# A block of two FFNs and a mixer on one Trainium2 core: half of x's quadrant sums move into the output projection, and the second FFN goes from four plain blocks and nine pairs to two and ten

## The chip, the core and the metric

The kernel runs on one core of a Trainium2 chip. The metric is device time in microseconds (us) of one execution, as the median of several runs; lower is better. The core has a matrix engine (PE, with its weight loads shown as PEld), VectorE (DVE), ScalarE (ACT), GpSimd (POOL) and SyncE (SP). Each works through its own queue in program order and waits on semaphores of the others; SP and POOL issue the DMAs here. Matrix products land in banks of PSUM; everything else lies in SBUF.

## What is computed

One layer on x of 512 tokens by 1024 features, float32: a half-weighted FFN, a mixer of two attentions, a second half-weighted FFN, and a norm.

```python
x = x + 0.5 * swiglu(rmsnorm(x, norm_ffn1), w_ffn1_gate, w_ffn1_up, w_ffn1_down)
x = x + hybrid_mixer(rmsnorm(x, norm_mix), w_in, ..., w_out, rel_bias)
x = x + 0.5 * swiglu(rmsnorm(x, norm_ffn2), w_ffn2_gate, w_ffn2_up, w_ffn2_down)
return rmsnorm(x, norm_final)
# swiglu(h, g, u, d) = (silu(h @ g) * (h @ u)) @ d, with 2816 hidden columns
```

## The kernel before

**Layout.** x is held transposed as eight tiles `x0` to `x7` of 128 features by 512 tokens. In the built program and in the trace they are `x_70` to `x_77`. Every factor of a product is split in two (`halves`, lines 76 to 93, and `halves_of_x`, line 210): ACT writes a rounded copy (`whi`, `sph`, `xo`, `th`), and the difference goes to `wlo`, `spl`, `xo`, `tl`. Three matmuls (`mm3`, lines 95 to 98) then stand for one product. The difference is taken by DVE, except for the weights loaded during the mixer, where POOL takes it in pieces of 128 columns (line 89).

**FFN.** The 2816 hidden columns are 22 blocks of 128. A *plain* block (line 244) multiplies gate and up weights with all 512 tokens: 48 matmuls of 512 columns. A *pair* (line 283) does two blocks at once by Strassen's scheme in Winograd's form. The weights are quartered by input half and block, x by input half and token half, and seven products of 24 matmuls with 256 columns replace eight. A pair's operands include sums of weight quarters (S1 to S4, DVE, line 299) and sums of x's quadrants (T1 to T4). The sums of x are the same for all pairs. `sums_of_x(k)` (line 192) makes them for k = 0 to 3 from the tiles `x[k]` and `x[k+4]`: ACT writes two gained copies into `xa`, DVE makes four sums into `xv`, and two splits follow, a narrow one of 256 columns for T1 and a wide one of 768 for the others. Plain blocks do not need them, so each FFN starts with four plain blocks, and the sums are made beside these (`begun`, line 441, after its steps 3, 7, 9 and 11). A pair's products add up in three PSUM banks `u`, `v`, `w`. The first product in `u` is copied away by ACT into `wc` (line 317), and the third product of the pair then adds onto the same bank.

**Norm.** The root of the mean square scales the FFN's results, not its input. For the second FFN POOL adds up the squares of x's tiles in `acc` (line 148); after step 2 PE sums them over features (`pr`), after step 4 it spreads the roots into rows (`pR`), and ACT copies these to `R` (line 167). Only then can a block be finished (`finish`, line 268, or `c12` and `c21`): two products with `R` on DVE, silu on ACT, a product, and the split into `h`.

**Down projection.** After a part of the hidden columns (`PARTS`, line 23) its down products are stepped in between the steps of later pairs, at places given by `SLOTS` and `FEWER` (`mixed`, line 398). After the first four blocks, eight down steps (`LEAD`) stand in one run before the pairs. A result tile in PSUM (`pd`) is added to x by DVE where its number is even. Where it is odd, ACT copies it to `acc`, and POOL sends a DMA that adds it to x (`half_sent`, line 495).

**Output projection.** `w_out` (line 845) multiplies the heads' outputs `oT` with `w_o` for eight tiles d, first k = 4 to 7 among the attention steps, then k = 0 to 3 at the end in the order 0, 1, 2, ... 7 (`last`, line 1067). Its PSUM tiles `pw` use the tag `mm`, which has two banks. `ended` (line 839) drains a bank: DVE adds it to x (line 840), then follow the gained split of x (`gained`, lines 132 and 133) and the square. Tiles 0 and 1 are held until the last head is done (`held`), and both finish together.

**Order.** PE's order is the order in which the program is written (`manual_schedule`). The queues of DVE, ACT, POOL and SP are set at build time by a scheduler that estimates durations. A tile from a pool (`tile_pool`) waits for the last user of what lay at its place. The mixer's pool for heads, `ap`, is closed with the mixer, and the FFN's pools are opened after that.

Of the kernel before, what the change touches and what calls it, by code (L numbers as in the profile page):

```python
# [21 lines left out]
PLAIN = 4  # L22
PARTS = (0, 4, 6, 10, 14, 18, 22)
# [5 lines left out]
LEAD = 8  # L29
AHEAD = ((0, 26.0, True), (0, 22.0, False), (1, 12.8, None), (2, 8.6, None))  # L30
SLOTS = (0, 1, 2, 3, 4, 5, 6, 7, 9, 12, 15, 18, 21, 23, 25, 27)
FEWER = (0, 1, 2, 3, 4, 5, 6, 7, 12, 16, 20, 24)


@with_exitstack
def block_kernel(ctx: ExitStack, tc: tile.TileContext, A: dict, out: bass.AP):
# [144 lines left out]
    class Ffn:  # L181


        def __init__(self, w, which, tmp, hp, sp):
            self.w, self.which, self.tmp, self.hp, self.sp = w, which, tmp, hp, sp
            self.xg, self.hs, self.early, self.cuts, self.halved = None, {}, {}, (), NF
            self.behind = made[0]
            self.t1 = [[xp.tile([128, S], F32R, name="xo", tag="xo", bufs=20) for _ in range(2)] for _ in range(2)]
            self.th, self.tl = [sp.tile([128, 4, 3, HT], F32R, name=n, tag=n, bufs=1) for n in ("th3", "tl3")]
            nc.gpsimd.memset(sp.tile([128, 16], F32, name="gap", tag="gap", bufs=1), 0.0)  # L190

        def sums_of_x(self, k):
            ab, v = [self.sp.tile([128, 4, 2, 128], F32, name=n, tag=t, bufs=3).rearrange("p a b c -> p (a b c)")
                     for n, t in (("xa", "sph"), ("xv", "spl"))]
# [6 lines left out]
            nc.vector.tensor_tensor(t1, a1, a2, ALU.subtract)  # L201
            nc.vector.scalar_tensor_tensor(t2, t1, -1.0, b2, ALU.mult, ALU.subtract)
            nc.vector.scalar_tensor_tensor(t4, t2, -1.0, b1, ALU.mult, ALU.subtract)
            nc.vector.tensor_tensor(t3, b2, a2, ALU.subtract)
# [78 lines left out]
        def pair(self, f):  # L283
# [9 lines left out]
            def sums(name):  # L293

                a11, a12, a21, a22 = [A[i, j] for i in range(2) for j in range(2)]
                to, x, y, op = {"S1": (a21, a21, a22, ALU.add), "S2": (a11, a21, a11, ALU.add),
                                "S3": (a11, a11, a22, ALU.subtract), "S4": (a12, a11, a12, ALU.add)}[name]
                with after(self.behind_lo):
                    nc.vector.tensor_tensor(to, x, y, op)  # L299
# [98 lines left out]
        def mixed(self, steps, fills):  # L398
# [103 lines left out]
    with ExitStack() as ph:  # L502
# [10 lines left out]
        ffn = Ffn(A["wgu1"], 0, tmp, hp, sp)  # L513
# [52 lines left out]
        def then(d, p):  # L566
# [13 lines left out]
        steps += ffn.mixed(pairs, fills) + ffn.down(A["wd1"][f:], fs, then, None, 4)  # L580
# [8 lines left out]
    with ExitStack() as ph:  # L589
        tmp = ph.enter_context(tc.tile_pool(name="tmp2", bufs=2))  # L590
        kv = ph.enter_context(tc.tile_pool(name="kv", bufs=1))
        ap = ph.enter_context(tc.tile_pool(name="ap", bufs=2))
# [244 lines left out]
        out_done = set()  # L837

        def ended(d, p, k0):
            nc.vector.tensor_tensor(xs[d], p, xs[d], ALU.add)  # L840
# [226 lines left out]
        last = [w_out(d, 0, 4, both if d < 2 else None) for d in range(NK)]  # L1067
# [66 lines left out]
        with tc.manual_schedule(engines={mybir.EngineType.PE}):  # L1134
            for i in range(len(steps) + 9):
# [9 lines left out]
        xg = [got["x", d] for d in range(NK)]  # L1145
# [3 lines left out]
    with ExitStack() as ph:  # L1149
        tmp = ph.enter_context(tc.tile_pool(name="tmp3", bufs=5))  # L1150
        hp = ph.enter_context(tc.tile_pool(name="hp3", bufs=2))
        sp = ph.enter_context(tc.tile_pool(name="sp3", bufs=2))
        ffn = Ffn(A["wgu2"], 2, tmp, hp, sp)
        ffn.xg = xg
        hs = ffn.hs
        ffn.halved = PARTS[-2]
# [4 lines left out]
        for f, end in zip(PARTS[1:], PARTS[2:]):  # L1161
# [4 lines left out]
        ffn.go(steps + ffn.mixed(pairs, fills))  # L1166
# [42 lines left out]
        last = range(PARTS[-2], NF)  # L1209
# [68 lines left out]
def _down(w):  # L1278
# [4 lines left out]
    for f, end in zip(PARTS, PARTS[1:]):  # L1283
# [5 lines left out]
def _laid_out(x, norm_ffn1, w_ffn1_gate, w_ffn1_up, w_ffn1_down, norm_mix, w_in, cmp_pos_k, cmp_w1_k,  # L1289
# [17 lines left out]
        "x": c(x[0]), "wd1": _down(w_ffn1_down[0]),  # L1307
# [6 lines left out]
        "wd2a": _down(w_ffn2_down[0])[:PARTS[-2]],  # L1314
        "wd2b": _blocks(w_ffn2_down[0][PARTS[-2] * 128:], F - PARTS[-2] * 128, S),
# [27 lines left out]
```

## Time and profile before

| | |
|---|---|
| median of 3 runs | 974.65 us (973.8 to 975.12) |
| profiled execution | 973.68 us, of which the span from first to last instruction is 971.9 us |
| mean granted PE clock | 0.999 |
| busy share of the span | PE 99%, PEld 88%, DVE 75%, ACT 55%, POOL 22% |
| last tiles of the output projection drained | 605.05 (x0, x1) to 625.62 us (x7) |
| first matmul of the second FFN | 622.04 us |
| first transpose of the tail (line 1178) | 940.23 us |

Times of trace rows are microseconds from the span's start. A timeline row gives start, duration, engine, line, operation, output and inputs, and in square brackets how long the engine stood idle before it and who released it. An operation that waits inside the engine shows it as a longer duration, with no bracket. Consecutive DVE and ACT operations start a little before the recorded end of the one ahead (the rows show 0.05 to 0.1 us).

### The profile page before, as it was taken

Reading aid. Unit: us, or ns where it says so; the run is one execution under the profiler, and the core shown is the slowest. Engines: PE = TensorE matmul, PEld = TensorE weight load, DVE = VectorE, ACT = ScalarE, POOL = GpSimd, SP = SyncE. Lnnn points to the kernel's source line nnn. Section 1 sums busy time; section 2 is a strip of 40 time slices with the busy share of each in tenths; the row PEclk is TensorE's granted clock in tenths of the full one; section 3 lists DMA queues with packets and bytes.
Section 4 is the critical chain, followed back from the end, with each engine's and each line's share of the span. In section 5 each row is a group of like instructions: output and inputs, shape, how many; then the busy total and the mean of one; then the engine's idle time right before and its main releaser. Section 6 shows DMA issues by size and latency. Waiting matters only on the chain.

```text
span 971.9 us, 16008 instructions
## 1 busy us (share of the span) xinstructions
PE 961.8 (99%) x6096; PEld 858.3 (88%) x6096; DVE 729.1 (75%) x1090; ACT 532.4 (55%) x893; POOL 217.8 (22%) x365
## 2 busy tenths in 40 slices
PE   9999999999999999999999999999999999999997
PEld 6889999999999898888888888888999999999986
DVE  5977787788776576678888885778678888777853
ACT  7844555454443445577676674674455554444534
POOL 0010010110001144236566564801001010100000
PEclk9999999999999999999999999999999999999999
DMA  8643574534532335662243531464446433445112
GB/s 311 241 136 93 173 223 137 157 107 105 135 83 65 85 101 163 202 195 62 70 109 98 131 99 54 152 216 120 121 119 163 127 97 115 118 132 153 44 22 87
DMA packets 51361, 124.39 MB, mean 128 GB/s; under 512 B 10673, under 2 KB 15234, under 8 KB 51284
## 3 DMA queue, kind: packets, MB, share of 16 engines
q1 hardware_dynamic: 39476, 91.62, 30.4%
q0 software_dynamic: 11520, 31.46, 13.5%
q8 instruction: 48, 0.79, 0.3%
q10 hardware_dynamic: 288, 0.27, 0.1%
q14 instruction: 29, 0.24, 0.1%
HBM read 100.08 MB, written 5.30 MB: 108 GB/s over the span
## 4 chain that ended last, share of the span: by engine, by line
PE 92%; DMA 3%; DVE 2%; issue 1%; POOL 1%; ACT 0%; SPq 0%; DVEq 0%; ACTq 0%
PE pd L97 8%; PE pd L96 8%; PE pd L98 8%; PE pu L98 7%; PE pu L97 7%; PE pu L96 7%; PE pw L96 5%; PE pw L97 5%; PE pw L98 5%; PE ps_t L976 3%; PE pv L96 3%; PE pv L98 3%; PE pv L97 3%; PE pp L96 3%; PE pgu L98 2%; PE pp L97 2%
## 5 line engine op out<-in xcount | busy, mean ns | idle before, releaser
L211 ACT ACTIVATE sph<-aw 128x1024 fp32r<-128x1024 f32 x128 | 133.7, 1059 | 147.1 <-PE pu L97 60.9
L212 DVE TENSOR_TENSOR spl<-aw,sph 128x1024 fp32r<-128x1024 f32 x128 | 155.0, 1223 | 57.2 <-ACT sph L211 57.1
L84 ACT ACTIVATE whi<-raw 128x1024 fp32r<-128x1024 f32 (+3 forms) x107 | 103.7, 971 | 98.9 <-PE pd L97 53.5
L500 POOL DMA_DIRECT2D x<-acc x40 | 35.0, 875 | 460.6 <-ACT acc L499 460.6
L96 PE MATMUL pd<-h,whi 128*128 128x512 f32 x320 | 126.5, 395 | 0.3 <-DVE x L493 0.3
L97 PE MATMUL pd<-h,whi 128*128 128x512 f32 x320 | 126.6, 396 | 0.0
L98 PE MATMUL pd<-h,wlo 128*128 128x512 f32 x320 | 125.8, 393 | 0.0
L91 DVE TENSOR_TENSOR wlo<-raw,whi 128x1024 fp32r<-128x1024 f32 (+3 forms) x83 | 102.9, 1243 | 28.0 <-ACT whi L84 27.3
L98 PE MATMUL pu<-th,spl 128*128 128x256 f32 x432 | 119.3, 276 | 0.0
L96 PE MATMUL pu<-th,sph 128*128 128x256 f32 x432 | 119.2, 276 | 0.0
L97 PE MATMUL pu<-tl,sph 128*128 128x256 f32 x432 | 119.2, 276 | 0.0
L299 DVE TENSOR_TENSOR aw<-aw 128x1024 f32<-128x1024 f32 x72 | 87.8, 1219 | 3.5 <-DMA aw<-in_wgu 3.2
L96 PEld LDWEIGHTS pu<-th,sph 128*128 128x128 f32 x432 | 81.1, 188 | 4.2
L97 PEld LDWEIGHTS pu<-tl,sph 128*128 128x128 f32 x432 | 81.1, 188 | 4.0
L98 PEld LDWEIGHTS pu<-th,spl 128*128 128x128 f32 x432 | 81.1, 188 | 0.0
L98 PE MATMUL pw<-xo,spl 128*128 128x256 f32 x288 | 79.6, 276 | 0.0
L96 PE MATMUL pw<-xo,sph 128*128 128x256 f32 x288 | 79.5, 276 | 0.0
L97 PE MATMUL pw<-xo,sph 128*128 128x256 f32 x288 | 79.5, 276 | 0.0
L89 POOL TENSOR_TENSOR wlo<-raw,whi 128x128 fp32r<-128x128 f32 x128 | 60.9, 508 | 60.8 <-DVE m L954 31.1
L98 PEld LDWEIGHTS pd<-h,wlo 128*128 128x128 f32 x320 | 60.1, 188 | 13.3
L96 PEld LDWEIGHTS pd<-h,whi 128*128 128x128 f32 x320 | 60.1, 188 | 3.8 <-DVE x L493 0.7
L97 PEld LDWEIGHTS pd<-h,whi 128*128 128x128 f32 x320 | 60.1, 188 | 2.5
(258 smaller groups left out, 2534.6 us busy)
## 6 DMA issues: line engine op xcount, KB each, us to landing
aw<-in_wgu SPq DMA_DIRECT2D x72, 512.0 KB, 4.8
raw<-in_wd POOLq DMA_DIRECT2D x22, 512.0 KB, 4.2
x<-acc POOLq DMA_DIRECT2D x40, 256.0 KB, 3.3
raw<-in_wd2a POOLq DMA_DIRECT2D x18, 512.0 KB, 4.1
raw<-in_w_a SPq DMA_DIRECT2D x16, 512.0 KB, 3.6
raw<-in_wgu SPq DMA_DIRECT2D x15, 512.0 KB, 4.3
raw<-in_w SPq DMA_DIRECT2D x8, 512.0 KB, 5.1
kvn<-xo SPq DMA_DIRECT2D x32, 128.0 KB, 2.4
```

What stands on the lines that cost most here:

```text
L84: nc.scalar.activation(hi[:, s], src[:, s], AF.Copy)
L89: nc.gpsimd.tensor_tensor(lo[:, i, b], src[:, i, b], f32(hi[:, i, b]), ALU.subtract)
L91: nc.vector.tensor_tensor(lo[:, s], src[:, s], f32(hi[:, s]), ALU.subtract)
L96: nc.tensor.matmul(p, w[0], v[0], start=first, stop=False, skip_group_check=again)
L97: nc.tensor.matmul(p, w[0], v[1], start=False, stop=False, skip_group_check=again)
L98: nc.tensor.matmul(p, w[1], v[0], start=False, stop=last, skip_group_check=again)
L211: nc.scalar.activation(hi, v, AF.Copy)
L212: nc.vector.tensor_tensor(lo, v, f32(hi), ALU.subtract)
L299: nc.vector.tensor_tensor(to, x, y, op)
L500: nc.gpsimd.dma_start(xs[d], acc, accum_op=ALU.add)
L976: nc.tensor.transpose(p[:, wide:wide + 128], lps[qi][:, j * 128:(j + 1) * 128], ident)
```

## The change

The second FFN has two plain blocks and ten pairs in place of four and nine; the first FFN stays as it is. The sums of x for k = 0 and 1 are made inside the output projection, as soon as tiles 4 and 5 are drained; those for k = 2 and 3 after the plain steps 3 and 2. To that end the end of the output projection runs in the order 0, 4, 1, 5, 2, 3, 6, 7 (0 and 4 held). `pR` comes after step 6 and not 4. No down steps stand in one run before the pairs, and the first part's down steps are put into the first pair from its step 8 on (`FIRST`). The mixer's head tiles go to the right end of SBUF and are given up before the last output tiles, so that `th3`, `tl3` and the copies `xa` and `xv` of the two early sums can lie there. The pool of the weights' tiles (`sp3`) is opened ahead of that for `h`.

```diff
-PLAIN = 4
-PARTS = (0, 4, 6, 10, 14, 18, 22)
+PARTS = ((0, 4, 6, 10, 14, 18, 22), (0, 2, 4, 6, 10, 14, 18, 22))
+FIRST = (8, 9, 10, 11, 12, 13, 14, 15, 17, 19, 21, 23)
...
-                if i % 28 in (FEWER if i < 84 else SLOTS) and fills and fills[0][0] <= i:
+                if i % 28 in slots[min(i // 28, len(slots) - 1)] and fills and fills[0][0] <= i:
...
-        sums = [(at, lambda k=k: ffn.sums_of_x(k)) for k, at in enumerate((3, 7, 9, 11))]
+        sums = [(at, lambda k=k: ffn.sums_of_x(k)) for k, at in sums]
...
-        return steps + fills[:LEAD], [(0, step) for step in fills[LEAD:]]
+        return steps + fills[:lead], [(0 if lead else 8, step) for step in fills[lead:]]
...
-        ap = ph.enter_context(tc.tile_pool(name="ap", bufs=2))
+        heads = ph.enter_context(ExitStack())
+        ap = heads.enter_context(tc.tile_pool(name="ap", bufs=2, side="right"))
...
                 squares(tmp, d, "t", 6)
+                later[d] = made[0]
+                if d in (4, 5):
+                    ffn.behind = later[d]
+                    ffn.sums_of_x(d % 4, xt)
...
-        last = [w_out(d, 0, 4, both if d < 2 else None) for d in range(NK)]
+        last = [w_out(d, 0, 4, both if d in (0, 4) else None) for d in (0, 4, 1, 5, 2, 3, 6, 7)]
...
+            heads.close()
+            tp = ctx.enter_context(tc.tile_pool(name="tp3", bufs=1, side="right"))
+            xt = ph.enter_context(tc.tile_pool(name="xt", bufs=2, side="right"))
+            ffn = Ffn(A["wgu2"], 2, tp)
             for _ in work:
                 pass
...
+        sp = ph.enter_context(tc.tile_pool(name="sp3", bufs=2))
         hp = ph.enter_context(tc.tile_pool(name="hp3", bufs=2))
-        sp = ph.enter_context(tc.tile_pool(name="sp3", bufs=2))
...
-            (2, lambda: roots(2, sums_of_squares("mm"))), (4, lambda: rows_of_roots(2, "mm"))])
+            (2, lambda: roots(2, sums_of_squares("mm"))), (6, lambda: rows_of_roots(2, "mm"))], 2, 0, ((2, 0), (3, 1)))
...
-        ffn.go(steps + ffn.mixed(pairs, fills))
+        ffn.go(steps + ffn.mixed(pairs, fills, (FIRST, FEWER, FEWER, FEWER, SLOTS)))
```

DVE's queue at the end of the output projection, before. `x<-pw` is the drain of a bank, `xo<-x,gcol,xo` the gained split.

```order
L840 TENSOR_TENSOR x_71<-pw,x_71 128x512
L133 SCALAR_TENSOR_TENSOR xo<-x_70,gcol,xo 128x512
L133 SCALAR_TENSOR_TENSOR xo<-x_71,gcol,xo 128x512
L840 TENSOR_TENSOR x_72<-pw,x_72 128x512
L133 SCALAR_TENSOR_TENSOR xo<-x_72,gcol,xo 128x512
L840 TENSOR_TENSOR x_73<-pw,x_73 128x512
L133 SCALAR_TENSOR_TENSOR xo<-x_73,gcol,xo 128x512
L840 TENSOR_TENSOR x_74<-pw,x_74 128x512
```

The same place now, from the third drain to the fifth. `xv` and `tl` rows belong to the sums of x for k = 0.

```order
L845 TENSOR_TENSOR x_71<-pw,x_71 128x512
L203 TENSOR_TENSOR xv<-xa 128x256
L206 TENSOR_TENSOR xv<-xa 128x256
L204 SCALAR_TENSOR_TENSOR xv<-xv,xa 128x256
L205 SCALAR_TENSOR_TENSOR xv<-xv,xa 128x256
L214 TENSOR_TENSOR xo<-xv,xo 128x256
L845 TENSOR_TENSOR x_75<-pw,x_75 128x512
L132 SCALAR_TENSOR_TENSOR xo<-x_71,gcol,xo 128x512
L214 TENSOR_TENSOR tl_6846<-xv,th_6845 128x768
L132 SCALAR_TENSOR_TENSOR xo<-x_75,gcol,xo 128x512
L845 TENSOR_TENSOR x_72<-pw,x_72 128x512
```

Between two drains stood one split; now five operations stand between the third and the fourth drain, three between the fourth and the fifth, and (not shown) four between the fifth and the sixth.

ACT's queue from the copy of `R` on, before: the first finished block follows at once, among sums of x.

```order
L167 ACTIVATE R<-pR 128x512
L272 ACT_TABLE_LOAD
L272 ACTIVATE t<-t 128x512
L84 ACTIVATE whi<-raw 128x1024
L231 ACTIVATE h<-t 128x512
```

The same place now: `sph` is a split of pair weights (ahead of `R` that of S2), `t` the silu of a plain block, `wc<-pu` the copy of the first pair's first product.

```order
L213 ACTIVATE sph<-aw 128x1024
L166 ACTIVATE R<-pR 128x512
L274 ACT_TABLE_LOAD
L274 ACTIVATE t<-t 128x512
L83 ACTIVATE whi<-raw 128x1024
L274 ACTIVATE t<-t 128x512
L233 ACTIVATE h<-t 128x512
L213 ACTIVATE sph<-aw 128x1024
L319 ACTIVATE wc<-pu 128x512
```

The copy of `R` and both blocks' silus now stand between the pair's first splits and the copy that its third product needs.

More of the change, by code (lines that the diff above doesn't have):

```diff
@@ L1 @@
 import math
-from contextlib import ExitStack
+from contextlib import ExitStack, nullcontext
 import concourse.bass as bass
@@ L181, in block_kernel, with __init__, works_in, sums_of_x @@
     class Ffn:
-        def __init__(self, w, which, tmp, hp, sp):
-            self.w, self.which, self.tmp, self.hp, self.sp = w, which, tmp, hp, sp
+        def __init__(self, w, which, tp):
+            self.w, self.which = w, which
             self.xg, self.hs, self.early, self.cuts, self.halved = None, {}, {}, (), NF
-            self.behind = made[0]
+            self.behind, self.behind_lo = made[0], None
             self.t1 = [[xp.tile([128, S], F32R, name="xo", tag="xo", bufs=20) for _ in range(2)] for _ in range(2)]
[L189 to L194, printed above, removed]
+            self.th, self.tl = [tp.tile([128, 4, 3, HT], F32R, name=n, tag=n, bufs=1) for n in ("th3", "tl3")]
+            nc.gpsimd.memset(tp.tile([128, 16], F32, name="gap", tag="gap", bufs=1), 0.0)
+        def works_in(self, tmp, hp, sp):
+            self.tmp, self.hp, self.sp = tmp, hp, sp
+        def sums_of_x(self, k, pool=None):
+            ab, v = [(pool or self.sp).tile([128, 4, 2, 128], F32, name=n, tag=t, bufs=2 if pool else 3).rearrange(
+                "p a b c -> p (a b c)") for n, t in (("xa", "sph"), ("xv", "spl"))]
             v = v.rearrange("p (a b) -> p a b", a=4)
@@ L297, in sums @@
                                 "S3": (a11, a11, a22, ALU.subtract), "S4": (a12, a11, a12, ALU.add)}[name]
-                with after(self.behind_lo):
+                with after(self.behind_lo) if self.behind_lo else nullcontext():
                     nc.vector.tensor_tensor(to, x, y, op)
@@ L396, in down, with mixed @@
             return steps
-        def mixed(self, steps, fills):
+        def mixed(self, steps, fills, slots):
             out, fills = [], list(fills)
@@ L438, in go, with begun @@
                     late()
-    def begun(ffn, w, posts):
-        steps = [s for f in range(0, PLAIN, 2) for s in ffn.plain(range(f, f + 2))]
-        sums = [(at, lambda k=k: ffn.sums_of_x(k)) for k, at in enumerate((3, 7, 9, 11))]
+    def begun(ffn, w, posts, plain, lead, sums):
+        steps = [s for f in range(0, plain, 2) for s in ffn.plain(range(f, f + 2))]
+        sums = [(at, lambda k=k: ffn.sums_of_x(k)) for k, at in sums]
         for at, post in posts + sums:
             steps[at].post.append(post)
-        fills = ffn.down(w, range(PLAIN), half_sent, "mm", 2)
-        return steps + fills[:LEAD], [(0, step) for step in fills[LEAD:]]
+        fills = ffn.down(w, range(plain), half_sent, "mm", 2)
+        return steps + fills[:lead], [(0 if lead else 8, step) for step in fills[lead:]]
     scr_t = dp.tile([16, 128, RVW], F32, name="scr_t")
@@ L572, in block_kernel @@
             (3, squares_of_tokens), (4, lambda: roots(0, ss[:, 0])), (5, lambda: rows_of_roots(0, "mm")),
-            (13, make_rows)])
+            (13, make_rows)], 4, 8, enumerate((3, 7, 9, 11)))
         pairs = []
-        for f, end in zip(PARTS[1:], PARTS[2:]):
+        for f, end in zip(PARTS[0][1:], PARTS[0][2:]):
             fs = range(f, end)
@@ L579, in block_kernel @@
                 fills += [(len(pairs) + 8, step) for step in ffn.down(A["wd1"][f:], fs, half_sent)]
-        steps += ffn.mixed(pairs, fills) + ffn.down(A["wd1"][f:], fs, then, None, 4)
+        steps += ffn.mixed(pairs, fills, (FEWER, FEWER, FEWER, SLOTS)) + ffn.down(A["wd1"][f:], fs, then, None, 4)
         pairs[20].post.append(put_rows)
@@ L837, in block_kernel @@
         out_done = set()
+        later = {}
         def ended(d, p, k0):
@@ L1207, in norm @@
                 queue.dma_start(out[i * 128:(i + 1) * 128, half * S:(half + 1) * S], y[half])
-        last = range(PARTS[-2], NF)
+        last = range(PARTS[1][-2], NF)
         w = []
@@ L1275, in _gate_up, with _down @@
     return np.ascontiguousarray(v.transpose(4, 3, 1, 2, 0, 5))
-def _down(w):
+def _down(w, parts):
     import numpy as np
@@ L1282, in _down @@
     chunks = []
-    for f, end in zip(PARTS, PARTS[1:]):
+    for f, end in zip(parts, parts[1:]):
         part = v[:, :, f:end]
```

19 lines of the change are left out of this document (9 added, 10 removed).

## The prediction

> **What bounds the kernel now.** I read the page first, then PE's waits, then timelines of the engines from the end of the output projection on, the only place where the two programs' orders differ ahead of the second FFN.
>
> ```profile
> span 971.9 us, 16008 instructions
> PE 961.8 (99%) x6096; PEld 858.3 (88%) x6096; DVE 729.1 (75%) x1090; ACT 532.4 (55%) x893; POOL 217.8 (22%) x365
> PE 92%; DMA 3%; DVE 2%; issue 1%; POOL 1%; ACT 0%; SPq 0%; DVEq 0%; ACTq 0%
> PE pd L96 <- DVE x L493: 0.3, 2, 0.2
> ```
>
> PE is busy 99% of the span and holds 92% of the chain that ended last. In the second FFN its waits view shows just 0.3 us, for two down banks. So matmuls taken away count in full, and every wait that the change makes for PE counts in full against them. Shares do not say whether it makes any: DVE's 75% is a mean over stages.
>
> ```profile
> 605.00:622.00 17.00, 16.91 (x75) 13.66 (x74) 11.08 (x14) 12.34 (x20) 16.34 (x24) 1.00 0.30 94
> ```
>
> This row gives busy time in one stretch, in the order PE, PEld, DVE, ACT, POOL. In the last 17 us of the output projection POOL is busy 16.34 and DVE 11.08. DVE seems to have 5.9 us free there, the room into which the change puts two sums of x.
>
> **Part 1: the matmuls.** The pitch of matmuls comes from the starts of a run of equal ones.
>
> ```profile
> 605.80 0.50 PE L96 MATMUL pw<-kvn,whi 128*128 128x512 f32 x1
> ...
> 616.15 0.39 PE L96 MATMUL pw<-kvn,whi 128*128 128x512 f32 x1
> ...
> 621.36 0.39 PE L98 MATMUL pw<-kvn,wlo 128*128 128x512 f32 x1
> ...
> 630.44 0.95 PE L154 MATMUL pr<-ones_f,acc 128*128 128x1 f32 x8
> 631.25 0.48 PE L96 MATMUL pgu<-xo,whi 128*128 128x512 f32 x1
> ```
> ```profile
> 754.73 0.28 PE L97 MATMUL pu<-tl,sph 128*128 128x256 f32 x1
> ...
> 756.54 0.28 PE L98 MATMUL pu<-xo,spl 128*128 128x256 f32 x1
> 756.66 0.40 PE L96 MATMUL pd<-h,whi 128*128 128x512 f32 x1
> ...
> 757.36 0.28 PE L96 MATMUL pu<-xo,sph 128*128 128x256 f32 x1
> ```
>
> 23 pitches in 5.21 us (616.15 to 621.36) are 0.2265 for 512 columns, 16 in 1.81 are 0.1131 for 256. Two plain blocks are 96 x 0.2265 = 21.74 us, a pair 168 x 0.1131 = 19.00: minus 2.74. The eight down steps that stood in one run now stand singly between pair steps, where one takes 0.70 (756.66 to 757.36) and not 3 x 0.2265 = 0.68: plus 0.16. Together **-2.58**, if PE waits for nothing new.
>
> **Part 2: the early sums.** Each `sums_of_x` issues on DVE four sums, a narrow and a wide split, on ACT two copies and two splits. They lie in DVE's queue ahead of drains of the two `mm` banks, so PE waits behind them once a drain is later than one tile's products, 12 x 0.2265 = 2.72 us. What they cost there:
>
> ```profile
> 591.81 1.71 POOL L89 TENSOR_TENSOR wlo<-raw,whi 128x128 fp32r<-128x128 f32 x4 [2.17 <-ACT whi L84]
> ...
> 605.65 4.29 POOL L89 TENSOR_TENSOR wlo<-raw,whi 128x128 fp32r<-128x128 f32 x8 [4.49 <-ACT whi L84]
> 609.91 1.29 POOL L148 TENSOR_TENSOR acc<-acc,sq 128x512 f32<-128x512 f32 x1
> 611.15 2.21 POOL L89 TENSOR_TENSOR wlo<-raw,whi 128x128 fp32r<-128x128 f32 x4
> ...
> 628.20 1.79 POOL L148 TENSOR_TENSOR acc<-acc,sq 128x512 f32<-128x512 f32 x1 [1.30 <-ACT sq L147]
> ```
> ```profile
> 605.05 1.39 DVE L840 TENSOR_TENSOR x<-pw,x 128x512 f32<-128x512 f32 x2 [0.83 <-PE pw L98]
> 606.93 0.99 DVE L133 SCALAR_TENSOR_TENSOR xo<-x,gcol,xo 128x512 fp32r<-128x512 f32 x1 [0.49 <-ACT xo L132]
> 608.58 1.04 DVE L133 SCALAR_TENSOR_TENSOR xo<-x,gcol,xo 128x512 fp32r<-128x512 f32 x1 [0.66 <-ACT xo L132]
> 609.55 0.68 DVE L840 TENSOR_TENSOR x<-pw,x 128x512 f32<-128x512 f32 x1
> ...
> 622.06 1.93 DVE L91 TENSOR_TENSOR wlo<-raw,whi 128x1024 fp32r<-128x1024 f32 x1
> 623.91 1.78 DVE L133 SCALAR_TENSOR_TENSOR xo<-x,gcol,xo 128x512 fp32r<-128x512 f32 x1
> ...
> 626.96 1.22 DVE L91 TENSOR_TENSOR wlo<-raw,whi 128x1024 fp32r<-128x1024 f32 x1 [0.66 <-ACT whi L84]
> 628.10 0.74 DVE L133 SCALAR_TENSOR_TENSOR xo<-x,gcol,xo 128x512 fp32r<-128x512 f32 x1
> 628.76 1.51 DVE L201 TENSOR_TENSOR xv<-xa 128x256 f32<-128x256 f32 x1
> 630.39 0.43 DVE L202 SCALAR_TENSOR_TENSOR xv<-xv,xa 128x256 f32<-128x256 f32 x1
> 630.73 0.42 DVE L204 TENSOR_TENSOR xv<-xa 128x256 f32<-128x256 f32 x1
> ...
> 632.87 0.95 DVE L212 TENSOR_TENSOR tl<-xv,th 128x768 fp32r<-128x768 f32 x1
> ```
>
> DVE and POOL work in turns when both have SBUF operands. A gained split takes 0.74 alone, 0.99 and 1.04 beside POOL's short pieces, 1.78 beside its additions of squares; a sum of 256 columns takes 0.42 alone and 1.51 beside an addition; POOL's own addition goes from 1.29 to 1.79, four of its pieces from 1.71 to 2.21. A drain, which reads PSUM, stays at 0.68. So meeting a piece costs DVE about 0.25, meeting an addition about 1.1. The row by windows says that POOL always has something to meet: per tile four pieces and one addition.
>
> The Trainium skill ("SBUF — State Buffer", section "SBUF: two separate sides") states that DVE operations with two SBUF inputs and GpSimd lock a shared port pair for the whole instruction. The rows agree on who waits, not on how long: at 606.93 the split lost 0.25, less than a piece's 0.43. By whole instructions a meeting would cost about 0.2 more (0.43 for 0.25, 1.29 for 1.1), an estimate from these rows, and with the twelve meetings of the walk below this part would come to 6.15 instead of 3.75.
>
> Now the walk. Up to the third drain at 609.55 DVE's queue has the same kinds of operations as before, so I start there. PE ends tile 5 at 605.8 + 2 x 2.72 = 611.2 and tile 2 at 614.0.
>
> - Between the third drain and that of tile 5 stand five operations of 256 columns: 5 x 0.34, one addition 1.1, three pieces 0.75, so it is drained at 613.1 to 613.8. PE asks for that bank at 614.0: no wait, by 0.2.
> - Then two gained splits and the wide split: 2 x 0.66 + 0.87, an addition 1.1 and two pieces 0.5, so tile 2 is drained at 617.5 to 618.1. PE has ended tile 3 at 616.7 and waits **1.4** for the bank.
> - Then four sums: 1.36, an addition 1.1, a piece or two 0.4, and tile 3 is drained at 621.7. PE ended tile 6 at 620.8: **0.85**. The FFN begins at 624.4, not 622.0.
> - Behind that drain stand a gained split 0.66, the narrow split 0.34 with an addition 1.1, and the first block's `wlo` 1.14 with an addition 1.1: it is done at 626.0. PE's third matmul of the FFN wants it at 624.9: **1.2**. Then the wide split, a drain and tile 3's gained split (0.87 + 0.6 + 0.66) end at 628.1, some 0.3 after PE's step wants it: **0.3**.
>
> Sum **+3.75**. Its bounds: 0 if DVE meets POOL only at its pieces, which takes 1.1 off the first three steps and 2.2 off the last; above, 0.2 more at each of the twelve meetings, 6.15.
>
> **Part 3: the first pair.** It begins at 624.4 + 1.5 (the waits) + 8 x 2.72 + 0.8 each for `pr` (630.44 to 631.25) and `pR`, which has as many matmuls = 649.3. The first two products need no sums of x and no `R`. The third, at 649.3 + 2 x 2.72 = 654.7, adds onto bank `u`, so ACT must have made the copy `wc`. In ACT's queue that copy stands behind the end of both plain blocks, and `R`'s row behind the split of S2.
>
> ```profile
> 637.91 0.60 ACT L167 ACTIVATE R<-pR 128x512 f32<-128x512 f32 x1 [2.68 <-PE pR L165]
> 638.52 1.28 ACT L272 ACT_TABLE_LOAD   x1
> 639.82 0.63 ACT L272 ACTIVATE t<-t 128x512 f32<-128x512 f32 x1
> ...
> 642.19 0.64 ACT L231 ACTIVATE h<-t 128x512 fp32r<-128x512 f32 x1 [0.69 <-DVE t L273]
> ...
> 678.47 1.06 ACT L211 ACTIVATE sph<-aw 128x1024 fp32r<-128x1024 f32 x1 [2.85 <-PE pu L97]
> 679.43 0.58 ACT L317 ACTIVATE wc<-pu 128x512 f32<-128x512 f32 x1
> ```
> ```profile
> aw<-in_wgu SPq DMA_DIRECT2D x6, 512.0 KB, 6.7
> ```
>
> The first pair's weights are asked for behind POOL's last addition, about 633.4 (two more additions and two gained splits after 628.1, in turns), and land 6.7 later (the row's median for issues from 600 to 680) at 640.1. ACT splits the first quarter in 1.0. Then DVE has, each at its spacing, five operations of 1024 columns up to S2's sum (two splits of quarters, one of down weights, two sums: 5 x 1.14), the last wide split 0.87, and about 1.5 of waits for ACT's roots with their table load of 1.28: S2 is ready near 649.3, ACT has split it at 650.4, and `R` is copied only then, though PE spread it before its last plain step. From `R`'s start ACT needs 0.52 + 1.28 + 2 silus at 0.54 + `whi` 0.96 + `h` 0.54 + a split 0.96 + `wc` 0.58, and 0.2 for DVE's product: 6.1. The copy is done at 656.5: PE waits **1.8**. Behind it the first down banks wait for ACT's `acc` and DVE's add, which stand behind the same heap: 0.9 and 0.4 by the same count, **+3.1** in all. Bounds: 0 if the weights land 3 us sooner, 5 if DVE is 2 us later still.
>
> **At nothing.** Four more half-sent tiles (24, not 20): ACT's 0.58 and DVE's 0.68 each lie beside PE; their spacing of four down steps, each beside a pair step (4 x 1.38 = 5.5), stays above copy and landing (0.58 + 3.3), and with less cover ACT would wait for the rest. The heads' tiles at the right: POOL's memset waits for the last head before eight pieces, where POOL stood idle 4.49 until 605.65. One gain: the two down waits (0.3) go with the rows they stood at, **-0.3**.
>
> ```profile
> x<-acc POOLq DMA_DIRECT2D x40, 256.0 KB, 3.3
> ```
>
> **Sum.** The profiled execution took 973.68: the span and 1.78 around it. 973.68 - 2.58 + 3.75 + 3.1 - 0.3 = 977.65. The median of the runs lies 0.97 above the profiled one, so I predict 978.6.
>
> **Rivals.**
>
> - *The cover holds (faster).* Place: the drain of tile 2 in the output projection and the copy `wc`. If DVE is through with tile 5's splits by 616.7 and `R` is copied by 648.6, PE waits for nothing and the time is 974.65 - 2.58 = 972.1. For it: DVE's 11.08 of 17 us. Against it: the 1.51 and 1.78 rows, and no idle time on POOL. Chance 0.13.
> - *One of two.* Only the output projection stalls (974.65 - 2.58 + 3.75 = 975.8), or only the first pair (975.2): DMAs may land sooner, or the additions fall beside drains. Chance 0.17.
> - *Longer meetings.* POOL and DVE exclude each other for whole instructions: 6.15 in place of 3.75, so 981.0. Against it: the loss of 0.25 at 606.93. Chance 0.07.
>
> **How the numbers follow.** The forecast keeps 0.63. Two tenths of a per cent, about what a measurement of this kernel tells from no change, are 1.95 us: the forecast and the longer meetings lie above (0.70), one of two within (0.17), the cover below (0.13). For eight in ten the range reaches from 973.2, the lowest of the single stalls (975.2 with 2 us less in the pair), to 981.0, where part 2 stands at its upper bound; the cover (0.13) is left out.
>
> **What would show it.** In the profile after: PE's or its weight loads' waits for DVE's `x<-pw` at about 617 and 621, DVE's `xv` rows near 1.5 us there, the first matmul of the FFN at 624.4, a wait for `wlo` behind it, then a wait of 1.8 for ACT's `wc<-pu` near 655. The whole should be 4 us longer. I am wrong if PE shows none of these; then DVE did not meet POOL, or the additions were not in its way.

## The result, and the profile after

| | before | after |
|---|---|---|
| median of the runs | 974.88 us (4 runs, 973.8 to 976.1) | 988.35 us (4 runs, 987.8 to 989.53) |
| profiled execution, span | 973.68, 971.9 | 989.53, 987.8 |
| first matmul of the output projection's last part | 599.16 | 601.59 |
| first matmul of the second FFN | 622.04 | 627.27 |
| first transpose of the tail | 940.07 (the table ahead of the prediction has 940.23) | 956.3 |

The ratio is 1.0139, with a 95% interval of 1.0122 to 1.0157: slower, as forecast, but by 13.5 us and not by 4, and outside the range that was given (973.2 to 981.0). The first lines of the page after, and PE's waits from the output projection on (what waited, for whom; us in total, times, longest):

```profile
span 987.8 us, 16182 instructions
PE 972.6 (98%) x6168; PEld 869.5 (88%) x6168; DVE 747.7 (76%) x1102; ACT 538.7 (55%) x904; POOL 221.2 (22%) x369
PE 86%; DVE 5%; DMA 4%; issue 2%; ACT 2%; POOL 0%; SPq 0%; DVEq 0%; ACTq 0%; POOLq 0%
```
```profile
PE pw L95 <- DVE x L845: 1.8, 3, 0.7
PE pd L95 <- ACT acc L501: 1.1, 2, 0.8
PE pgu L97 <- DVE wlo L90: 0.8, 1, 0.8
PE pu L95 <- ACT wc L319: 0.5, 1, 0.5
PE pu L95 <- DVE t L338: 0.3, 1, 0.3
```

All the forecast waits are there: the banks of the output projection, `wlo`, `wc`, `acc`. But they come to 4.5 us, and PE is busy 10.8 us longer than before (972.6 against 961.8) although part 1 of the forecast takes work away. Busy time that grows while work shrinks points to slower instructions. So I compared the same matmuls at the same place, first by a view of groups between 700 and 900 us (count, busy us, mean ns of one), with the row of that window (x is the number of matmuls). Of before:

```profile
L98 PE MATMUL pw<-xo,spl 128*128 128x256 f32 x112 | 30.9, 276 | 0.0
700.00:900.00 200.00, 200.00 (x1456) 1.00 0.45 124
```

And of after, with two rows of the timeline (start, us) that give the pitch as well:

```profile
L97 PE MATMUL pw<-xo,spl 128*128 128x256 f32 x104 | 29.4, 282 | 0.0
700.00:900.00 200.00, 199.70 (x1407) 1.00 0.44 121
```
```profile
845.16 0.28 PE L95 MATMUL pu<-th,sph 128*128 128x256 f32 x1
...
847.32 0.39 PE L95 MATMUL pd<-h,whi 128*128 128x512 f32 x1
```

Eighteen matmuls of 256 columns run between the last two starts: 2.16 / 18 = 0.120 us each, where the forecast's rows of before gave 0.1131. The mean of one grows by the same 6 ns, and PE starts 1407 matmuls where it started 1456, at the same granted clock (1.00) and with 0.3 us idle, room for three of the 49 that are missing. Ten pairs have 1680 such matmuls: 1680 x 0.006 = 10 us. That is the part that the forecast lacks. What the change did to these matmuls is only their operands' place: in the second FFN the pair weights `sph` moved from byte 175488 of each partition to 142656 and `th3` from 150848 to 204704 (addresses are those of the built programs). x's tiles `xo` stayed at 27968 and on.

### The profile page after: what moved, and what is told of

It reads as the page before. It is cut to its first block, busy times and chain, and to the rows that moved or that the text cites. A ratio compares the mean times of both kernels' runs of the same rounds, so it can differ in the third digit from the quotient of the medians.

```text
span 987.8 us, 16182 instructions
## 1 busy us (share of the span) xinstructions
PE 972.6 (98%) x6168; PEld 869.5 (88%) x6168; DVE 747.7 (76%) x1102; ACT 538.7 (55%) x904; POOL 221.2 (22%) x369
## 4 chain that ended last, share of the span: by engine, by line
PE 86%; DVE 5%; DMA 4%; issue 2%; ACT 2%; POOL 0%; SPq 0%; DVEq 0%; ACTq 0%; POOLq 0%
PE pd L95 8%; PE pd L96 8%; PE pd L97 8%; PE pu L95 7%; PE pu L97 7%; PE pu L96 7%; PE pw L95 4%; PE pw L96 4%; PE pw L97 4%; PE pv L96 3%; PE pv L95 3%; PE pv L97 3%; PE pp L95 3%; PE pp L96 3%; PE ps_t L985 3%; PE pp L97 3%
## 5 line engine op out<-in xcount | busy, mean ns | idle before, releaser
L213 ACT ACTIVATE sph<-aw 128x1024 fp32r<-128x1024 f32 x135 | 140.6, 1057 | 155.5 <-PE pu L96 60.6
L214 DVE TENSOR_TENSOR spl<-aw,sph 128x1024 fp32r<-128x1024 f32 x135 | 163.2, 1222 | 60.4 <-ACT sph L213 60.1
L95 PE MATMUL pu<-th,sph 128*128 128x256 f32 x456 | 127.6, 280 | 1.4 <-DVE t L338 0.9
L96 PE MATMUL pu<-tl,sph 128*128 128x256 f32 x456 | 127.4, 279 | 0.0
L97 PE MATMUL pu<-th,spl 128*128 128x256 f32 x456 | 127.3, 279 | 0.0
L90 DVE TENSOR_TENSOR wlo<-raw,whi 128x1024 fp32r<-128x1024 f32 (+3 forms) x79 | 98.2, 1246 | 25.1 <-ACT whi L83 24.8
L301 DVE TENSOR_TENSOR aw<-aw 128x1024 f32<-128x1024 f32 x76 | 92.5, 1218 | 8.7 <-DMA aw<-in_wgu 8.4
L97 PEld LDWEIGHTS pu<-th,spl 128*128 128x128 f32 x456 | 85.9, 188 | 0.0
L97 PE MATMUL pw<-xo,spl 128*128 128x256 f32 x304 | 85.0, 279 | 0.0
L96 PE MATMUL pw<-xo,sph 128*128 128x256 f32 x304 | 84.9, 279 | 0.0
L95 PE MATMUL pw<-xo,sph 128*128 128x256 f32 x304 | 84.8, 279 | 0.0
```

The costliest lines, as they stand in the source:

```text
L90: nc.vector.tensor_tensor(lo[:, s], src[:, s], f32(hi[:, s]), ALU.subtract)
L95: nc.tensor.matmul(p, w[0], v[0], start=first, stop=False, skip_group_check=again)
L96: nc.tensor.matmul(p, w[0], v[1], start=False, stop=False, skip_group_check=again)
L97: nc.tensor.matmul(p, w[1], v[0], start=False, stop=last, skip_group_check=again)
L213: nc.scalar.activation(hi, v, AF.Copy)
L214: nc.vector.tensor_tensor(lo, v, f32(hi), ALU.subtract)
```

## The experiments

Theory A: the address of the pair weights sets the pitch. Rivals: B, the address of `th3` and `tl3`; C, ten pairs or the traffic beside them, with addresses of no account. A ratio is always to the kernel before on the same chip, with its 95% interval.

**Which address.** The first kernel puts 64 unused bytes ahead of the weights' pool and of `h`'s:

```diff
         sp = ph.enter_context(tc.tile_pool(name="sp3", bufs=2))
+        nc.gpsimd.memset(sp.tile([128, 16], F32, name="pad1", tag="pad1", bufs=1), 0.0)
         hp = ph.enter_context(tc.tile_pool(name="hp3", bufs=2))
+        nc.gpsimd.memset(hp.tile([128, 16], F32, name="pad2", tag="pad2", bufs=1), 0.0)
```

> The changed kernel, with an unused 64-byte tile ahead of the pool of the pair weights (sph, spl) in the second FFN and one ahead of the pool of h: the weights then lie at 142720 bytes of each partition and on (a multiple of 128, as in the kernel before, where they were at 175488) instead of 142656 (64 over a multiple of 128); th3 and tl3 stay at 204704 and 216992. Theory A (the weights' address sets the pace of the 256-column matmuls): the pitch falls from 0.119 to 0.113 us, 1680 of them give 10 us back, 978.4. Theory B (the address of the moving th3 and tl3 sets it): 988.4. Theory C (neither; ten pairs, or what runs beside them, slow the matmuls): 988.4.

Measured: 983.27, ratio 1.0087 (1.0072 to 1.0102), about half of what theory A gave. The second moves `th3` and `tl3` (`[128, 16]` of `gap` becomes `[128, 40 if which else 16]`):

> The changed kernel, with th3 and tl3 96 bytes further left, at 204608 and 216896: 64 over a multiple of 128 as in the kernel before (150848), not 32 over as in the changed one (204704). The weights stay at 142656. Theory A: 988.4. Theory B: 978.4, if all 1680 matmuls follow, or 983.4 if only the 960 that read th3 and tl3 do (960 x 0.006 = 5.8). Theory C: 988.4.

Measured: 987.31, 1.0132 (1.0117 to 1.0147). The third is the kernel before without its `gap`:

```diff
-            nc.gpsimd.memset(sp.tile([128, 16], F32, name="gap", tag="gap", bufs=1), 0.0)
+            if not which:
+                nc.gpsimd.memset(sp.tile([128, 16], F32, name="gap", tag="gap", bufs=1), 0.0)
```

> The kernel before, without the 64-byte tile that stands ahead of the pair weights in the second FFN: the weights (sph, spl) move from 175488 to 175424 bytes, so from a multiple of 128 to 64 over one; th3 stays at 150848, nothing else changes in order or number. Theory A: nine pairs of 168 matmuls x 0.006 us = +9.1, 984.0. Theory B and theory C: 974.9, as the kernel before.

Measured: 982.76, 1.0085 (1.0068 to 1.0102). The fourth has both moves:

> The changed kernel with both moves: weights at 142720 (a multiple of 128) and th3 and tl3 at 204608 and 216896 (64 over). Theory A: 978.4, as with the weights' move alone. Theory B: 978.4, where the weights' move alone gave 988.4. Theory C: 988.4. If both addresses count, this one is the fastest of the three.

Measured: 980.20, 1.0060 (1.0045 to 1.0075). The same two lines as above, of the third and of the fourth:

```profile
L98 PE MATMUL pw<-xo,spl 128*128 128x256 f32 x104 | 29.4, 283 | 0.0
700.00:900.00 200.00, 200.00 (x1410) 1.00 0.42 117
```
```profile
L97 PE MATMUL pw<-xo,spl 128*128 128x256 f32 x112 | 31.0, 277 | 0.0
700.00:900.00 200.00, 199.96 (x1450) 1.00 0.46 126
```

The third settles it against C: nothing changes but 64 bytes ahead of the weights (and the memset that fills them), and the matmuls are as slow (283 ns) as in the changed kernel. A holds for the larger part: of the 7.7 us that both moves give back, the weights' move alone gives 5.1. `th3` has a part too, mostly with the weights right (1.0087 to 1.0060), hardly without (1.0139 to 1.0132).

**The parts of the change, with these addresses put right.** Four plain blocks and nine pairs, with the early sums:

```diff
-PARTS = ((0, 4, 6, 10, 14, 18, 22), (0, 2, 4, 6, 10, 14, 18, 22))
+PARTS = ((0, 4, 6, 10, 14, 18, 22), (0, 4, 6, 10, 14, 18, 22))
...
-            (2, lambda: roots(2, sums_of_squares("mm"))), (6, lambda: rows_of_roots(2, "mm"))], 2, 0, ((2, 0), (3, 1)))
+            (2, lambda: roots(2, sums_of_squares("mm"))), (4, lambda: rows_of_roots(2, "mm"))], 4, 8, ((2, 9), (3, 11)))
...
```

> The changed kernel with both tiles' addresses put right (as in the fastest of the first four), but with four plain blocks and nine pairs in the second FFN: the two early sums, the order of the output projection and the layout alone. Forecast's part 2: 974.1 + 3.75, and 1512 matmuls that still take 0.001 us longer, +1.5: 979.4. If the early sums are covered: 975.6.

Measured: 979.90, 1.0063 (1.0044 to 1.0083). Without the early sums as well (all four made beside the plain blocks, as in before):

```diff
-                if d in (4, 5):
-                    ffn.behind = later[d]
-                    ffn.sums_of_x(d % 4, xt)
...
-        last = [w_out(d, 0, 4, both if d in (0, 4) else None) for d in (0, 4, 1, 5, 2, 3, 6, 7)]
+        last = [w_out(d, 0, 4, both if d < 2 else None) for d in range(NK)]
...
```

> As the one ahead, without the early sums: all four sums of x beside the four plain blocks, the output projection in its old order. What is left of the change is the place of the tiles (heads' tiles, th3 and tl3 at the right end, the weights' pool ahead of that for h), with the addresses put right. If the layout costs nothing but the 0.001 us for each of 1512 matmuls: 975.6. If the heads' tiles at the right cost the mixer 2 us, as the changed kernel's profile had it: 977.6. If the addresses are right: 974.1.

Measured: 975.53, 1.0017 (1.0008 to 1.0027). PE's waits view from the output projection on is empty in this one; with the early sums it has

```profile
PE pw L95 <- DVE x L845: 1.8, 3, 0.7
PE pgu L97 <- DVE wlo L90: 0.8, 1, 0.8
```

the two waits of the forecast's part 2 and no others. So the early sums cost 0.0046 of 974.35, 4.5 us, give or take 2 (3.75 forecast). Ten pairs instead of nine, with the first pair's waits, are the step from 1.0063 to 1.0060: -0.3 us, with an uncertainty of about 2 (+0.2 forecast).

Is it POOL's additions that DVE meets? The next kernel leaves out seven of them, and with them the seven squares that ACT makes for them (`if d == 0:` ahead of `squares(tmp, d, "t", 6)`):

> The changed kernel with both addresses put right, without POOL's additions of squares in the output projection (the squares of tile 0 alone stand for all eight; seven squares on ACT and seven additions on POOL are left out). Theory of the forecast (DVE loses 1.1 us at each addition it meets): the waits for banks (2.75) and for the first down weights' difference (1.2) go, and some of the first pair's, 980.2 - 3.95 = 976.2 or less. Rival (DVE's queue is too long by itself): the waits stay, 980.

Measured: 974.70, 1.0010 (1.0001 to 1.0020), by the ratios 4.9 us less than with both addresses right. ACT has less to do there too. In the next kernel ACT's squares stay, and only the additions go to DVE:

```diff
-                squares(tmp, d, "t", 6)
+                squares(tmp, d, "t", 6, nc.vector)
```

> The changed kernel with both tiles' addresses put right, and the seven additions of squares in the output projection on DVE and not on POOL (nothing is left out). If DVE loses 1.1 us at each addition of POOL that it meets, and an addition of its own takes 0.68: about half of the 5.5 us that leaving them out gave, 977.5, down to 975.5 where its own additions fall beside idle time. If the additions only lengthened DVE's queue: 980.2 or more.

Measured: 976.66, 1.0024 (1.0013 to 1.0035). DVE now does more work itself and PE waits less. The rows say why. DVE's in the changed kernel, the two additions of POOL that its slow sums meet there, and then DVE's rows here (start, us):

```profile
611.97 0.68 DVE L845 TENSOR_TENSOR x<-pw,x 128x512 f32<-128x512 f32 x1
612.57 1.33 DVE L203 TENSOR_TENSOR xv<-xa 128x256 f32<-128x256 f32 x1
613.83 0.68 DVE L206 TENSOR_TENSOR xv<-xa 128x256 f32<-128x256 f32 x1
...
620.95 1.52 DVE L206 TENSOR_TENSOR xv<-xa 128x256 f32<-128x256 f32 x1
...
626.31 2.31 DVE L90 TENSOR_TENSOR wlo<-raw,whi 128x1024 fp32r<-128x1024 f32 x1
```
```profile
612.33 1.29 POOL L147 TENSOR_TENSOR acc<-acc,sq 128x512 f32<-128x512 f32 x1
...
620.71 1.48 POOL L147 TENSOR_TENSOR acc<-acc,sq 128x512 f32<-128x512 f32 x1
```
```profile
611.50 0.51 DVE L203 TENSOR_TENSOR xv<-xa 128x256 f32<-128x256 f32 x1
611.93 0.68 DVE L206 TENSOR_TENSOR xv<-xa 128x256 f32<-128x256 f32 x1
612.53 0.68 DVE L204 SCALAR_TENSOR_TENSOR xv<-xv,xa 128x256 f32<-128x256 f32 x1
613.14 0.95 DVE L147 TENSOR_TENSOR acc<-acc,sq 128x512 f32<-128x512 f32 x1
```

A sum of 256 columns takes 0.42 alone (the prediction's row), 0.68 beside a piece, 1.33 or 1.52 beside an addition. The drain ahead stays at 0.68. Both slow sums start 0.24 after POOL's addition and end 0.28 after its end (613.90 against 613.62, 622.47 against 622.19). An addition of DVE's own is 0.68 to 0.95: mostly less than the 0.9 to 1.1 that meeting one of POOL's costs, and POOL's queue is shorter besides.

**What rule the addresses follow.** The reading so far was "the weights must lie 64 over a multiple of 128 from the moving tile". The fifth kernel asks whether it is the distance or the place, with a longer pad among the constants (`PAD + 16`), so that everything moves:

> The kernel before with a pad tile among the constants 64 bytes longer, so that everything behind it lies 64 bytes further up: x's tiles at 28032 in place of 27968, th3 at 150912, the pair weights at 175552 (second FFN) and 200128 (first FFN). The distances between weights and moving tiles stay, the weights' own address goes from a multiple of 128 to 64 over one in both FFNs. If the weights' address by itself decides: twice nine pairs at 0.119 us, 2 x 8.6 = +17, 991.3. If the distance between the two streams decides: 974.1, as before.

Measured: 974.08, 0.9996 (0.9986 to 1.0005): so this move of 64 alone does not matter, and distances do. Then the rule was put to `h`, with `pad1` (16 columns) in `h`'s pools and `pad2` (16) behind:

> The kernel before with h, the moving tiles of the down products, 64 bytes further up in both FFNs (118144 in place of 118080; the weights whi and wlo of these products lie at 81216 and on, 64 over a multiple of 128, as h did); two 64-byte tiles are added so that the distance of the pair weights to x and th3 stays a 64 over a multiple of 128. The down matmuls have a pitch of 0.232 to 0.233 us in the trace of before, plain ones of the same 512 columns 0.2267. If a distance of 64 over a multiple of 128 is what all matmuls want: 960 x 0.0055 = -5.3, 969.0. If the rule holds only for matmuls of 256 columns: 974.3.

Measured: 987.04, 1.0119 (1.0104 to 1.0134). And to the plain weights, with 16 columns ahead of `raw`:

> The kernel before with the pool of all plain, down and mixer weights (raw, whi, wlo) 64 bytes further up: whi at 81280, a multiple of 128, while x's tiles and h stay 64 over one (h at 118208); one more 64-byte tile keeps what lies behind in its old distances. If all matmuls want the distance of 64: as with h alone, and the mixer's products of 512 columns (0.228 to 0.232 now) gain too, 967 to 969. If only matmuls of 256 columns do: 974.3.

Measured: 990.08, 1.0150 (1.0133 to 1.0167). Both expectations failed, in the direction too: the rule is wrong. In both the pairs had moved by 128, which that rule calls nothing. Three kernels took it apart. `h` alone (`pad1` of 16 columns, `pad2` of 112, so that the rest moves by 512):

> The kernel before with h alone 64 bytes further up modulo 512, in both FFNs: h at 118144, then 448 bytes more, so that th3, tl3, the pair weights, aw and wc move by 512. If h's place slowed the pairs when it was moved before: 987, with 0.118 a matmul. If the weights' distance to x (192) did: 974.5, with 0.1134.

Measured: 977.57, 1.0037 (1.0021 to 1.0052), between the two expectations. The pairs' tiles by 128 (`pad2` of 32 columns):

> The kernel before with th3, tl3, the pair weights, aw and wc 128 bytes further up in both FFNs and h where it was. Distance of the weights to x's tiles 192, to th3 64 as before (modulo 512). If the weights' distance to the moving tile of the same matmul decides: x's matmuls slow (0.118), th3's and tl3's fast, half of +12.5: 981. If the earlier run's slow th3 matmuls came with h: as here, 981. If the place of th3, weights and x together decides, all are slow: 987.

Measured: 984.87, 1.0108 (1.0091 to 1.0125), and x's and `th3`'s matmuls are slow alike. The pair weights by 512 (`gap` of 144 columns):

> The kernel before with the pair weights, aw and wc 512 bytes further up in both FFNs, th3, h and x where they were. If the distance counts modulo 512: 974.5 and 0.1134 a matmul. If a longer period or the address itself counts: slower, up to 992 (two FFNs at 0.119).

Measured: 974.49, 0.9997 (0.9983 to 1.0012). Last, the plain weights (112 columns ahead of `raw`, 16 behind):

> The kernel before with raw, whi and wlo 448 bytes further up and all that lies behind 512, so modulo 512 only these weights move, by -64. Their distance to h is then 448, as where h alone moved by 64 and down matmuls took 0.229 for 0.232 to 0.233; the distance of the pair weights to h and x stays. If distances alone decide, and plain matmuls stay at 0.227: 960 x 0.004 = -3.8, 970.8. If plain matmuls and the mixer's take 0.233, as where these weights moved by +64: 760 x 0.006 = +4.6 on top, 975.4. If the pairs slow too: over 980.

Measured: 986.18, 1.0124 (1.0099 to 1.0149): the pairs slow down although no pair matmul reads a tile whose distance to the others it reads has changed (modulo 512). The two lines of the window from 700 to 900 us for the last three, in the order told (pairs by 128, weights by 512, plain weights):

```profile
L98 PE MATMUL pw<-xo,spl 128*128 128x256 f32 x107 | 29.9, 280 | 0.0
700.00:900.00 200.00, 200.00 (x1428) 1.00 0.42 117
```
```profile
L98 PE MATMUL pw<-xo,spl 128*128 128x256 f32 x112 | 30.9, 276 | 0.0
700.00:900.00 200.00, 200.00 (x1458) 1.00 0.44 124
```
```profile
L99 PE MATMUL pw<-xo,spl 128*128 128x256 f32 x105 | 29.5, 281 | 0.0
700.00:900.00 200.00, 200.00 (x1417) 1.00 0.42 115
```

The second keeps 276 ns, the others do not. All kernels together, with the distance of each tile from x's tiles modulo 512, in the second FFN (the mean is that of `pw<-xo,spl`):

| kernel | `th3` | pair weights | `h` | `whi` | mean ns | matmuls, 700 to 900 us |
|---|---|---|---|---|---|---|
| before; all 64 up; weights 512 up | 0 | 64 | 0 | 0 | 276 | 1456, 1458, 1458 |
| the last three versions, below | 0 | 64 | 0 | 0 | 276 | 1458, 1454, 1448 (0.7 us idle) |
| both put right, and the four kernels made from it | 0 | 64 | 128 | 0 | 277 | 1445 to 1453 |
| `h` alone | 0 | 64 | 64 | 0 | 277 | 1447 |
| weights put right | 96 | 64 | 128 | 0 | 277 | 1437 |
| pairs by 128 | 128 | 192 | 0 | 0 | 280 | 1428 |
| `h` and pairs | 128 | 192 | 64 | 0 | 280 | 1425 |
| plain weights up, all behind by 128 | 128 | 192 | 128 | 64 | 279 | 1428 |
| plain weights down | 0 | 64 | 0 | 448 | 281 | 1417 |
| before without `gap`; `th3` put right | 0 | 0 | 0 | 0 | 283 | 1410, 1410 |
| after | 96 | 0 | 0 | 0 | 282 | 1407 |

Kernels with the same distances agree to within ten, whatever else differs in them (nine or ten pairs, left or right end), and every row that differs from the first has a longer mean, by 1 to 7 ns. So the pace goes with the place of several tiles together, and a rule for one pair of tiles does not do. Tiles that PE does not read moved along with these (`raw`, `aw`, `wc`), so the runs do not show that PE's own reads alone count. That 512 is the period is not shown either: a move of 512 costs nothing and one of 128 does, but one of 256 was not made.

The starts of PE's rows between 700 and 900 us tell more. In before, one matmul of 256 columns follows another after 0.1125 us where DVE, ACT and POOL all stand idle (106 spacings) and after 0.113 where DVE and ACT both work; in before without `gap` it is 0.1196 (103) and 0.119. Of the spacings beside idle engines, some 40 in each kernel lie where the DMA engines were busy for less than a tenth of the time, and these have the same means, 0.1125 and 0.120. So neither the other engines nor the DMA have to work at that moment for PE to be slow. Between 655 and 930 us, with `h` alone moved, the spacing is 0.118 in the first four matmuls behind a down step and 0.113 from the thirteenth on; with the plain weights down it is 0.117 near a down step and far from it.

**The change with every address as before.** `h` put right too, the additions on DVE, and later down steps:

```diff
-FIRST = (8, 9, 10, 11, 12, 13, 14, 15, 17, 19, 21, 23)
+FIRST = (10, 11, 12, 13, 15, 17, 18, 19, 21, 22, 23, 25)
...
-        nc.gpsimd.memset(hp.tile([128, 16], F32, name="pad2", tag="pad2", bufs=1), 0.0)
+        nc.gpsimd.memset(hp.tile([128, 112], F32, name="pad2", tag="pad2", bufs=1), 0.0)
```

> The one with the squares added on DVE, with two more edits. h lies 384 bytes further up (171840), so that every tile of the second FFN has the same address modulo 512 as in the kernel before. The first part's down steps start in the first pair at its step 10 and not 8, and stand less close (waits of 1.4, 0.5 and 1.2 there). If h's place holds the remaining 0.001 us a matmul: pitch 0.1134 and -1.7; if the later down steps find h and the sending tile ready: -2 of the 3.0. Both: 976.7 - 3.7 = 973.0; only the steps: 974.7; neither: 976.7.

Measured: 975.02, 1.0003 (0.9993 to 1.0013). Pitch and waits went as expected, and all that is left in the waits view is the first row here, with the rows of the pair matmuls behind it:

```profile
PE pw L95 <- DVE x L845: 0.5, 1, 0.5
```
```profile
L97 PE MATMUL pw<-xo,spl 128*128 128x256 f32 x110 | 30.4, 276 | 0.0
700.00:900.00 200.00, 200.00 (x1458) 1.00 0.46 127
```

Of the 2 us that are missing against the expectation, all could lie in the mixer: in the profile it took 253.7 us (347.5 to 601.3), and 251.7 in before. Its heads' tiles lay 992 bytes off their old place, 480 modulo 512. So 480 bytes more went into their pool (`pad3`, 120 columns):

> The last version of the changed kernel (all addresses of the second FFN as before modulo 512, squares on DVE, later down steps) with 480 bytes more in the pool of the heads' tiles, so that these too have their old addresses modulo 512 (lp at 213312, before 212800). If their address costs the mixer 2 us (253.7 in the trace of that version, 251.7 in before): 973.0. If it is an event that comes and goes in the same kernel: 975.0.

Measured: 974.61, 0.9990 (0.9980 to 1.0000). The mixer took 251.7. With the heads' tiles off their old place, the profiles of nine kernels had 251.9 to 253.7; with these and the mixer's weights in their old place modulo 512, those of nine others, before among them, had 251.6 to 252.2. The two ranges overlap, with one profile of each kernel, and so do the intervals of the ratios (1.0003 and 0.9990). A cost of up to 2 us for the place of the heads' tiles is likely, and not shown. Last, the down steps wider apart, `FIRST = (10, 11, 13, 15, 17, 18, 20, 22, 24, 26)`:

> The last version with the heads' tiles put right too, and the first part's down steps set wider apart in the first pair (ten in it, six in the second), against the wait of 0.7 us for the tile that ACT sends. If that wait goes and nothing takes its place: 0.7 us less than 0.9990 of the kernel before, 0.9983, about 973.5 beside a kernel before at 975. If it only moves into the second pair: 0.9990.

Measured: 973.47, 0.9992 (0.9983 to 1.0001). The wait moved: 0.7 for DVE's `t` in the place of 0.7 for ACT's `acc`.

```profile
PE pu L95 <- DVE t L338: 0.7, 1, 0.7
PE pw L95 <- DVE x L845: 0.5, 1, 0.5
```

Both last versions are 0.8 to 1.0 us below the kernel before, at the edge of what these runs can tell. They beat the changed kernel by over 14 us.

## Why the prediction was wrong

**The step that failed** is the paragraph "At nothing", and with it the pitch in part 1. It counted the heads' tiles at the right end as free, said nothing of where the pair weights, `th3` and `h` would lie, and took 0.1131 us a matmul from before as if it belonged to the matmul. It belonged to the addresses: with them the pitch was 0.120. Measured, the placement costs 7.7 us in the second FFN (1.0139 against 1.0060) and 1.7 more, give or take 1, with the layout alone (1.0017: pair matmuls still 1 ns longer, 1512 x 0.001 = 1.5, and perhaps the mixer's tiles). A hint stands in the code: a 64-byte tile that nobody reads, which the change moved to another pool. I did not ask what it was for.

The other steps, by their numbers:

| step | forecast | measured |
|---|---|---|
| part 1, ten pairs for nine, at equal pitch | -2.58 | -2.4 with `h` right and no wait there: from the FFN's first matmul to the tail's first transpose 315.7 us (625.4 to 941.1), before 318.1, of which 0.3 are the two down waits |
| part 2, early sums | +3.75 | +4.5 by the ratios, give or take 2; 2.8 + 0.8 = 3.6 by the rows |
| FFN begins later | 2.35 | 2.8 (25.7 us from the last part of the projection, before 22.9) |
| wait for `wlo` | 1.2 | 0.8 |
| wait for `wc` | 1.8 | 0.5 after, 1.0 with addresses right |
| first down banks | 0.9 + 0.4 | 1.1 after, 1.4 with addresses right |
| parts 1 and 3 and the two down waits | +0.2 | -0.3, give or take 2 |
| place of the tiles | 0 | 7.7 + 1.7 = +9.4 |
| sum, ratio by ratio | +4 | +13.6 |

- Part 1 holds, once the addresses are equal. The row counts only came out of a kernel in which nothing waits in the second FFN; in the last two versions, each with one wait of 0.7, it is 317.1 and 316.4.
- Part 2 holds in mechanism and nearly in size. Three banks came late, not two: 617.06, 620.76 and 624.42, with idle times of 0.41, 0.73 and 0.69 in the rows

```profile
617.06 0.47 PE L95 MATMUL pw<-kvn,whi 128*128 128x512 f32 x1 [0.41 <-DVE x L845]
...
620.76 0.47 PE L95 MATMUL pw<-kvn,whi 128*128 128x512 f32 x1 [0.73 <-DVE x L845]
...
624.42 0.47 PE L95 MATMUL pw<-kvn,whi 128*128 128x512 f32 x1 [0.69 <-DVE x L845]
```

  The lateness is spread, since the tile order lets one bank's delay push the next. That POOL's additions are the cause is shown: with them on DVE 3.5 us go, and 4.9 where they and ACT's squares are left out. The price for a meeting, 0.25 a piece and 1.1 an addition, was met by the rows (0.68 - 0.42 and 1.33 or 1.52 - 0.42). The rival of whole-instruction meetings had 6.15 for this part; 3.6 and 4.5 lie nearer to the forecast, though the ratios alone would allow 6.15. The Trainium skill ("SBUF — State Buffer", section "SBUF: two separate sides") has that rule of a lock for the whole instruction. The rows with additions agree with it, since both slow sums end 0.28 after POOL's addition does. The prediction held the smaller loss beside a piece against that rule, and this does not follow: an operation that comes while a piece is under way waits only for what is left of it, so a loss of 0.26 beside a piece of 0.43 fits as well. What was too high in the rival is its price, a whole POOL instruction at every meeting.
- Part 3 holds as a chain (`R`, table load, `wc`, `acc`), in waits that are smaller than forecast: 2.4 us in all with the addresses right, where 3.1 stood. That parts 1 and 3 together came to -0.3 where +0.2 was forecast is in part luck: the measurement leaves 2 us either way. The copy `wc` was done at 658.6 in the profile after, 2.1 later than forecast, and the pair began 3.0 later (652.3):

```profile
652.57 0.58 ACT L166 ACTIVATE R<-pR 128x512 f32<-128x512 f32 x1
...
658.03 0.57 ACT L319 ACTIVATE wc<-pu 128x512 f32<-128x512 f32 x1
```

- The rivals were all about waits. None had PE itself slower, and so the range ended at 981.0. With the addresses right the change stands at 980.20, inside it: what was forecast was the change's order, and not its layout.

Why these distances matter is not settled. Two things were shown: the same distances give the same pace in different kernels, and moving a tile that among the second FFN's pairs only the down steps read slows the pair matmuls too (`whi` with `raw` and `wlo`: 276 to 281 ns; `h`: 0.113 to 0.118 us in the first matmuls behind a down step). A meeting with accesses of ACT, DVE, POOL or the DMA does not fit, since PE is as slow where these stood idle (0.120). Two streams of PE's own that meet at the same part of SBUF would fit; no run here shows which.

## What to carry to other kernels

When a change opens, closes or reorders pools, compare the tiles' addresses of both builds before anything else, and count nothing as free that moves a tile which the busiest engine reads. If the mean of one instruction of an unchanged kind differs between two profiles at the same clock, look for a place, not for a wait: pad the tile back to its old distance and take the time again. Where two engines share a path, moving the smaller work onto the engine that is waited for can be cheaper than leaving it beside it.

## What the hardware showed that I had not expected

- PE's pitch at 256 columns is 0.113 us or up to 0.120 at a granted clock of 1.00, by the tiles' addresses alone (64 bytes in the kernel before: a mean of one of 276 against 283 ns, a span of 971.9 against 981.0 us). The Trainium skill ("SBUF — State Buffer", section "SBUF: two separate sides") says that PE never waits on anyone at its ports, and gives it a read port of its own for the weights. That PE is as slow beside idle engines as beside busy ones (0.1196 and 0.119 us) agrees with the first. But neither accounts for the measured loss of 6 ns in 113, which stands without any wait in the view; where it arises is not shown.
- Products of 512 columns have it too: between 20 and 50 us, among the plain blocks of the first FFN, 389 ns in the mean of one in before and 395 with `whi` 64 bytes further up. The pitch there is 0.227 and 0.234 us.

```profile
L97 PE MATMUL pgu<-xo,whi 128*128 128x512 f32 x43 | 16.7, 389 | 0.0
```
```profile
L98 PE MATMUL pgu<-xo,whi 128*128 128x512 f32 x42 | 16.6, 395 | 0.0
```

- The distance that suits one is not that of the other: of the distances that were tried, the pairs ran fastest with 64 between weights and moving tile, plain products with 0 between `whi` and x's tiles.
